# Average pooling by four: loads of 8 MiB with 64 KiB runs in two buffers, in place of 4 MiB with 32 KiB runs in four, and the wait for stores on the load queue

## Chip, cores, metric

One core of one Trainium2 chip. The metric is device time in microseconds (us), the median over several executions. In the profile's lines DVE is VectorE, ACT is ScalarE and POOL is GpSimd; SPq and ACTq are the queues on which SyncE and ScalarE issue DMAs; L70 is line 70 of that run's kernel.

## The reference

```python
x: (64, 256, 8192) float32, kernel_size = stride = 4
out[:, :, i] = mean(x[:, :, 4*i : 4*i+4], axis=2)      # (64, 256, 2048)
```

The program reads 536.87 MB and writes 134.22 MB. It has 16384 rows of 8192 numbers. Both kernels treat them as 32 groups of 128 partitions x 4 rows, so that the four rows of one partition lie next to each other in memory (128 KiB in, 32 KiB out).

## The kernel before

One row per partition is one load of 4 MiB (a 32 KiB run on each of 128 partitions). Four such buffers take the loads in turn. VectorE sums four numbers at a time, ScalarE multiplies by 1/4 in place, and when the four rows of a group are done, one store of 4 MiB (again 32 KiB per partition) goes out from ScalarE's queue. There are two result buffers of one group each, so before the first row of group g is written, the store of group g-2 must have landed: **VectorE** waits for that.

```python
# F = 4 rows per group, _NIN = 4 input buffers, _NOUT = 2 result buffers
def load(i):                                   # on SyncE's queue
    ld = nc.sync.dma_start(out=xbuf(i), in_=xrow(i))          # 128 x 32 KiB
    if i >= _NIN:
        ld._wait_ge(s_dve, i - _NIN + 1)       # buffer given back by VectorE
    ld.then_inc(s_in[i % _NIN], 16)
...
for i in range(NR):                            # VectorE
    g, f = divmod(i, F)
    if f == 0 and g >= _NOUT:
        nc.vector.wait_ge(s_out[g % _NOUT], 16 * (g // _NOUT))   # store g-2 landed
    nc.vector.tensor_reduce(out=..., in_=xbuf(i)..., op=add)
for i in range(NR):                            # ScalarE
    nc.scalar.mul(o, o, inv_k)._wait_ge(s_dve, i + 1).then_inc(s_act, 1)
    if g < NG - 2 and f == F - 1:
        store(nc.scalar, g)                    # 128 x 32 KiB
# ... the last two stores are shared between the two queues, the very last one cut in two
```

## Time and profile before

| | before |
|---|---|
| time | 1559.98 us (1559.95 to 1560.06, 3 runs) |
| DMA | 671.12 MB at a mean of 431 GB/s |
| VectorE / ScalarE busy | 71% / 16% |
| one group (4 loads + 1 store), steady | 48.5 us |

The page of the kernel before: busy time by engine, then the span in 40 slices (DMA is the busy share of the 16 DMA engines in tenths, 9 means 90% or more), the DMA queues (q1 is SyncE's, q10 is ScalarE's, q14 carries instructions; packets, MB, share of the engines' time), the chain of work that ended last, VectorE's reductions (busy us, mean ns of one, idle before them), and the DMA issues (KB each, median us from issue to landing).

```profile
DVE 1111.8 (71%) x128; ACT 245.7 (16%) x129; POOL 0.2 (0%) x4
...
DMA  9999999999999999999999999999999999999999
GB/s 407 427 431 431 431 435 435 436 431 431 431 431 435 434 434 431 431 431 431 434 437 433 431 431 431 431 437 434 434 431 431 431 431 436 434 434 431 431 431 392
DMA packets 23187, 671.12 MB, mean 431 GB/s; under 512 B 2576, under 2 KB 2576, under 8 KB 2576
...
q1 hardware_dynamic: 18720, 542.12, 80.8%
q10 hardware_dynamic: 4464, 128.98, 19.2%
q14 instruction: 3, 0.02, 0.0%
...
DMA 81%; DVE 18%; ACT 0%; issue 0%; SPq 0%
...
L92 DVE TENSOR_REDUCE res<-xin 128x2048 f32<-128x8192 f32 x128 | 1111.8, 8686 | 434.5 <-DMA xin<-in_x_dram 434.5
...
xin<-in_x_dram SPq DMA_DIRECT2D x128, 4096.0 KB, 39.8
out_dram<-res ACTq DMA_DIRECT2D x30, 4096.0 KB, 23.2
```

No slice drops below nine tenths, and the rate hardly moves: the DMA engines are the limit. The last two lines are the median times from issue to landing: 39.8 us for a load (it queues behind others) and 23.2 us for a store.

The whole waits of the DMA queue on SyncE, and of VectorE, in the kernel before (waiter, line, releaser: us in total, times, longest):

```profile
SPq L70 <- DVE res L92: 1462.3, 124, 18.9
```

```profile
DVE res L92 <- DMA xin<-in_x_dram: 434.5, 128, 13.0
```

The loads wait only for VectorE to give buffers back, and VectorE waits only for loads. The wait for the stores shows up nowhere: it is always over when it is reached.

**The packets.** The trace also records each DMA packet (start, duration, size, queue). In this trace one packet is one run of one partition: 32 KiB for loads and stores. I strung the packets together into 16 DMA engines by the rule that each starts where the previous one of its engine ended. On one of them, where a load and a store are both queued, it reads as follows. (This is my listing from the trace's records, start in us from the span's start, then duration.)

```
105.40 load 32 KiB 1213 ns     109.03 store 32 KiB 1213 ns
106.61 store 32 KiB 1213 ns    110.24 load 32 KiB 1213 ns
107.82 load 32 KiB 1213 ns     111.45 store 32 KiB 1213 ns
```

Most packets start 1.209 or 1.210 us after the one before. The Trainium skill (the notes on the chip), page "DMA: Bandwidth & Descriptors", section "Where 436 GB/s comes from", gives 435.2 GB/s as the ceiling, which is an estimated 1.205 us per 32 KiB and engine (435.2 GB/s shared by 16 engines); this trace is within 0.4% of it. A group needs 32 load and 8 store packets per engine, 40 x 1.209 = 48.4 us, against a measured period of 48.5 us. The same page, section "Queues, rings and completion order", says that each engine goes round-robin over the queues at packet granularity; the listing shows it, with a turn of exactly one 32 KiB packet.

### The profile page before, as it was taken

The numbers are of one execution on the slowest core, as the hardware profiler recorded it, in microseconds if no ns is written. First come the engines' busy times: TensorE is split into PE (matmuls) and PEld (weight loads), VectorE is DVE, ScalarE is ACT, GpSimd is POOL, SyncE is SP. The second block draws the span as 40 slices with busy tenths as digits, with TensorE's granted clock in tenths as the row PEclk, the third lists the DMA queues.
The fourth block names the chain that finished last, engine by engine and source line by source line (L and its number), as shares of the span: only waits on it lengthen the run. The fifth ranks groups of instructions, "written<-read, shape, count | busy, mean of one in ns | idle before, by whom it ended". The sixth has DMA issues, their size and how long they took to land.

```text
span 1558.4 us, 501 instructions
## 1 busy us (share of the span) xinstructions
DVE 1111.8 (71%) x128; ACT 245.7 (16%) x129; POOL 0.2 (0%) x4
## 2 busy tenths in 40 slices
DVE  6767667686677866777666776667866677666786
ACT  1111111111111111111111111111111111111111
POOL 0000000000000000000000000000000000000000
DMA  9999999999999999999999999999999999999999
GB/s 407 427 431 431 431 435 435 436 431 431 431 431 435 434 434 431 431 431 431 434 437 433 431 431 431 431 437 434 434 431 431 431 431 436 434 434 431 431 431 392
DMA packets 23187, 671.12 MB, mean 431 GB/s; under 512 B 2576, under 2 KB 2576, under 8 KB 2576
## 3 DMA queue, kind: packets, MB, share of 16 engines
q1 hardware_dynamic: 18720, 542.12, 80.8%
q10 hardware_dynamic: 4464, 128.98, 19.2%
q14 instruction: 3, 0.02, 0.0%
HBM read 536.87 MB, written 134.22 MB: 431 GB/s over the span
## 4 chain that ended last, share of the span: by engine, by line
DMA 81%; DVE 18%; ACT 0%; issue 0%; SPq 0%
DMA xin<-in_x_dram 81%; DVE res L92 18%; ACT res L102 0%; SPq L70 0%; SPq L140 0%; SPq L67 0%
## 5 line engine op out<-in xcount | busy, mean ns | idle before, releaser
L92 DVE TENSOR_REDUCE res<-xin 128x2048 f32<-128x8192 f32 x128 | 1111.8, 8686 | 434.5 <-DMA xin<-in_x_dram 434.5
L102 ACT ACTIVATE res<-res 128x2048 f32<-128x2048 f32 x128 | 244.4, 1909 | 1301.7 <-DVE res L92 1301.7
L102 ACT ACT_TABLE_LOAD x1 | 1.3, 1283 | 0.9 <-SPq L67 0.9
L126 POOL MEMSET const-bfloat16-1.0<- 128x1 bf16 x1 | 0.1, 101 | 0.0
L126 POOL MEMSET const-uint8-127<- 128x1 uint8 x1 | 0.1, 101 | 0.0
L126 POOL MEMSET const-float32-0.0<- 128x1 f32 x1 | 0.1, 98 | 0.2 <-issue 0.2
L126 POOL MEMSET const-float32-1.0<- 128x1 f32 x1 | 0.1, 98 | 0.0
## 6 DMA issues: line engine op xcount, KB each, us to landing
xin<-in_x_dram SPq DMA_DIRECT2D x128, 4096.0 KB, 39.8
out_dram<-res ACTq DMA_DIRECT2D x30, 4096.0 KB, 23.2
out_dram<-res SPq DMA_DIRECT2D x1, 4096.0 KB, 42.4
out_dram<-res ACTq DMA_DIRECT2D x1, 3072.0 KB, 16.6
out_dram<-res SPq DMA_DIRECT2D x1, 1024.0 KB, 8.7
```

Source lines behind the costliest of these rows:

```text
L92: nc.vector.tensor_reduce(out=obuf(g)[:, f * OL : (f + 1) * OL], in_=xbuf(i).rearrange("p (m k) -> p m k", k=K), axis=mybir.AxisListType.X ...
L102: nc.scalar.mul(o, o, inv_k)._wait_ge(s_dve, i + 1).then_inc(s_act, 1)
L126: nc = _bacc.Bacc("TRN2", target_bir_lowering=False, num_devices=1)
```

## The change

Intent: fewer and larger loads (8 MiB, 64 KiB per partition, so two rows per load), and fewer instructions. The kernel keeps two input buffers of 64 KiB per partition, the same bytes as the four before. To keep VectorE's instructions down, a wait moves off it: the load queue now waits for the store of group g-2 before it issues the first load of group g. Every second tile is summed in two passes of pairwise adds (in place into the input buffer, then into the results), which takes VectorE less time than one pass.

```diff
-_NIN = 4
+_R = 2          # rows per load
+_NIN = 2
...
-            ld = nc.sync.dma_start(out=xbuf(i), in_=xrow(i))
-            if i >= _NIN:
-                ld._wait_ge(s_dve, i - _NIN + 1)
-            ld.then_inc(s_in[i % _NIN], 16)
+            g, j = divmod(t, G)                       # G = 2 tiles per group
+            if j == 0 and r0 == 0 and g >= _NOUT:
+                nc.sync.wait_ge(s_out[g % _NOUT], 16 * (g // _NOUT))
+            ld = nc.sync.dma_start(
+                out=xbuf(t, r0, r1),
+                in_=xview(g)[:, (j * R + r0) * L : (j * R + r1) * L],
+            )
+            if t >= _NIN:
+                ld._wait_ge(s_dve, t - _NIN + 1)
+            ld.then_inc(s_last if r0 > 0 else s_in[t % _NIN], 16)
...
-            if f == 0 and g >= _NOUT:
-                nc.vector.wait_ge(s_out[g % _NOUT], 16 * (g // _NOUT))
-            nc.vector.tensor_reduce(...)              # one row
+            elif t % G == 0:
+                nc.vector.tensor_reduce(...)          # two rows, one pass
+            else:
+                half = xbuf(t)[:, : T // 2]
+                pairs(half, xbuf(t))._wait_ge(s_in[t % _NIN], landed).then_inc(s_half, 1)
+                pairs(obuf(t), half)._wait_ge(s_half, t // G + 1).then_inc(s_dve, 1)
# ... (cut: the last tile is still loaded and summed row by row; ScalarE multiplies two rows at a time)
```

## The prediction

> **What bounds the kernel now.** DMA. The page's slices show the DMA engines at nine tenths or more throughout and 431 to 437 GB/s; the chain that ended last is 81% loads and 18% VectorE. In order of time that chain repeats every 48.5 us (91.47, 139.95, 188.44 ...): one group of four 4 MiB loads and one 4 MiB store. VectorE is 71% busy (reductions of 8686 ns), ScalarE 16%; both wait on loads. The trace's single DMA packets explain the period: 32 KiB takes 1.21 us on each of 16 engines; 40 packets per engine and group make 48.4 us. The Trainium skill, "DMA: Bandwidth & Descriptors" (Where 436 GB/s comes from), gives a ceiling of 435.2 GB/s; this trace sits within 1% of it. So nothing more than about 10 us can be won.
>
> **What the change does.**
> - Loads of 64 KiB packets: a 32 KiB packet takes 1.209 us, 1.205 at the ceiling; halving the count saves an estimated 2 to 3 us in all. Fewer instructions save the instruction fetches; two of the three (544 and 581 us) stretched their periods by under 1 us together.
> - VectorE per 8 MiB: one pass an estimated 17.2 us (twice 8686 ns, less one fixed cost), two passes 8.7 + 4.4 = 13.1 us [...]. Both are under the 19.3 us of an 8 MiB load: VectorE stays off the bottleneck, even with two buffers.
> - The wait for the store of two groups back moves from VectorE (just before the overwriting) to the load queue, one whole load earlier: load 2g+4 can't be issued before store g has landed.
>
> **Why that matters.** Packets of load and store queues alternate one for one on an engine where both have work (trace: 1.21 us load, 1.21 us store, in turn), so a 4 MiB store lands 23.2 us after issue (median, part 6). The skill's page (Queues, rings and completion order) says that engines switch queues by packets; here a packet is one 32 KiB descriptor. If a 64 KiB run stays one packet, a turn is 2.41 + 1.21 us, and eight store packets take 29 us instead of 19.3.
>
> Timeline, A = landing of load 2g+1: VectorE done A+13.3, ScalarE A+17, store issued; first store packet 4 to 7 us later (4.4 now), behind packets already taken. Load 2g+3 started at about A+19, so the store ends with or after it. By then the load queue is empty: load 2g+4 waits for the store's semaphore, then needs about 0.4 us receipt, 1.2 to 1.6 us from issue to first packet, and 0.7 us of first-packet delay (seen at the kernel's start). Estimate: 1.3 to 3.3 us of idle DMA per group, 30 times: 40 to 100 us, all critical. Startup and tail add about 7 us.
>
> **Predicted:** 1628 us, range 1566 to 1658. Chances: faster 0.02, within 2% 0.20, slower 0.78.
>
> **What would show it.** DMA share of slices falls to about 0.95, GB/s to about 412; period 50 to 52 us per group; the load queue's own waits name the store (out_dram<-res) on the group-opening loads; store issue-to-landing rises from 23 to about 30 us; loads have about half the packets (some 8,200 of data); VectorE reductions 17.2 us, adds 8.7 and 4.4 us, VectorE busy falling to about 975 us.
>
> **What would make it wrong.** If 64 KiB runs are cut to 32 KiB packets, or turns go by bytes, the store lands in about 23 us, well before load 2g+4 is due, and the time is 1558 to 1570. If fewer packets are taken ahead, the idle halves (about 1600). If adds at step two run slower than one element a cycle, VectorE adds more.

## The result

The changed kernel took **1634.32 us** (1633.09 to 1637.35, 4 runs) against 1560.02 us (4 runs) in the same rounds. The ratio is 1.0479 (95% interval 1.0461 to 1.0497): slower. A ratio here is the mean time of one kernel's fast runs over that of the other's fast runs of the same rounds, so it is not quite the ratio of the medians quoted.

The page of the changed kernel, with the lines that answer to those shown of before, and the three VectorE groups (busy us, mean ns, idle before them):

```profile
DVE 974.9 (60%) x96; ACT 232.9 (14%) x66; POOL 0.2 (0%) x4
...
DMA  9989999999999999999899999999999999999999
GB/s 411 411 362 435 411 411 426 410 424 397 426 424 386 435 400 411 425 398 437 363 434 424 386 434 402 411 424 394 442 386 419 422 393 437 411 411 415 408 423 374
DMA packets 14115, 671.12 MB, mean 411 GB/s; under 512 B 1568, under 2 KB 1568, under 8 KB 1568
...
q1 hardware_dynamic: 9648, 542.12, 79.4%
q10 hardware_dynamic: 4464, 128.98, 18.4%
q14 instruction: 3, 0.02, 0.0%
...
DMA 73%; DVE 26%; ACT 0%; issue 0%; SPq 0%
...
L134 DVE TENSOR_REDUCE res<-xin 128x4096 f32<-128x16384 f32 x32 | 551.0, 17220 | 297.1 <-DMA xin<-in_x_dram 297.1
L105 DVE TENSOR_TENSOR xin<-xin 128x8192 f32<-128x8192 f32 x31 | 269.5, 8692 | 350.0 <-DMA xin<-in_x_dram 350.0
...
L105 DVE TENSOR_TENSOR res<-xin 128x4096 f32<-128x4096 f32 x31 | 137.2, 4425 | 1.1
...
out_dram<-res ACTq DMA_DIRECT2D x30, 4096.0 KB, 32.8
```

The same bytes move at 411 instead of 431 GB/s, and the rate swings from slice to slice. VectorE does less work than before (975 against 1112 us), so it isn't VectorE's throughput. A store now takes 32.8 us to land instead of 23.2. The share of busy DMA barely falls, because a packet that is held up counts as busy; the rate tells more here than the share.

The load queue's own waits, after:

```profile
SPq L81 <- DMA out_dram<-res: 1087.1, 30, 39.4
SPq L82 <- DVE res L105: 432.5, 31, 15.3
```

Line 81 is the moved wait. The loads now wait mainly for stores. A wait on the issuing queue costs nothing by itself (run e2 below waits 799 us and hardly loses by it); what counts is whether the DMA engines run dry meanwhile. That can be seen where the wait ends. The timeline of the changed kernel around one such place (start, duration, engine, line, work; in brackets the idle time before):

```profile
702.67 8.69 DVE L105 TENSOR_TENSOR xin<-xin 128x8192 f32<-128x8192 f32 x1 [12.38 <-DMA xin<-in_x_dram]
702.89 0.33 SPq L82 DMA_DIRECT2D xin<-in_x_dram  x1
```

At 702.67 VectorE starts on a load that has just landed; it was the last one in flight. The next load is issued only at 702.89, although its buffer had been free since 690.29, when the reduction on it ended. The packets and landings of one DMA engine around it (my listing from the trace's records, as above):

```
694.98 load 64 KiB 2418 ns
697.39 store 32 KiB 1213 ns
698.60 load 64 KiB 2418 ns      last packet of that load
701.02 store 32 KiB 1213 ns     last packet of the store, ends 702.23
702.65    load has landed (all 16 engines)
702.83    store has landed -> 702.89 next load issued
703.86 load 64 KiB 2961 ns      1.63 us without a packet, then a slow first one
 ...
718.90 load 64 KiB 2434 ns
719.50    the next store is issued
721.33 load 64 KiB 3765 ns      held up 1.35 us
725.09 store 32 KiB 1213 ns     first packet of that store
726.30 store 32 KiB 1213 ns
727.51 load 64 KiB 2418 ns
```

Loads and stores still take turns one packet for one packet, but a load packet is now twice as long. In these turns the eight store packets of a group stretch over eight load packets, which is a whole load. So store and load finish together, and the queue is empty while the store's landing, the issue and the first packet follow one another.

Added up over the whole trace, mean of the 16 DMA engines (the packets at their usual duration, the gaps over 50 ns between packets, and the excess of packets over the usual duration):

| | packets at usual length | gaps | excess in long packets | one group, steady |
|---|---|---|---|---|
| before | 1548.2 us | 0.0 us | 4.0 us | 48.53 us |
| after | 1546.0 us | 35.2 us | 45.4 us | 50.79 us |

Of the excess after, 11.3 us are the slow first packets behind a gap, and 28.2 us are the packets just before a store's first one (30 of them, 0.94 us each). So the stalled queue costs about 35.2 + 11.3 = 46 us, and the start of the stores about 28 us. This splits the loss by place, not by cause: in e1 below, without the wait, the part before a store's first packet falls from 28 to 12 us as well. From the trace, 15 of the 16.4 gaps per engine lie between a store packet and the first packets of a group's first load, the load that waits for the store. The periods alternate, 52.1 and 49.2 us: a stalled group delays its loads, so that the next store starts earlier in them and ends in time; one engine had 16 gaps in 32 groups. The "one group" column is the mean distance of 28 store issues.

### The profile page after: what moved, and what is told of

It reads as the page before. It is cut to its first block, busy times and chain, and to the rows that moved or that the text cites. A ratio compares the mean times of both kernels' runs of the same rounds, so it can differ in the third digit from the quotient of the medians.

```text
span 1631.3 us, 343 instructions
## 1 busy us (share of the span) xinstructions
DVE 974.9 (60%) x96; ACT 232.9 (14%) x66; POOL 0.2 (0%) x4
## 4 chain that ended last, share of the span: by engine, by line
DMA 73%; DVE 26%; ACT 0%; issue 0%; SPq 0%
DMA xin<-in_x_dram 71%; DVE xin L105 16%; DVE res L105 8%; DMA out_dram<-res 2%; DVE res L134 1%; DVE res L125 1%; ACT res L152 0%; SPq L82 0%; SPq L192 0%; SPq L81 0%; SPq L75 0%
## 5 line engine op out<-in xcount | busy, mean ns | idle before, releaser
L134 DVE TENSOR_REDUCE res<-xin 128x4096 f32<-128x16384 f32 x32 | 551.0, 17220 | 297.1 <-DMA xin<-in_x_dram 297.1
L105 DVE TENSOR_TENSOR xin<-xin 128x8192 f32<-128x8192 f32 x31 | 269.5, 8692 | 350.0 <-DMA xin<-in_x_dram 350.0
L152 ACT ACTIVATE res<-res 128x4096 f32<-128x4096 f32 (+1 forms) x65 | 231.6, 3564 | 1391.1 <-DVE res L134 733.9
L105 DVE TENSOR_TENSOR res<-xin 128x4096 f32<-128x4096 f32 x31 | 137.2, 4425 | 1.1
L125 DVE TENSOR_REDUCE res<-xin 128x2048 f32<-128x8192 f32 x2 | 17.3, 8676 | 0.0
## 6 DMA issues: line engine op xcount, KB each, us to landing
out_dram<-res ACTq DMA_DIRECT2D x30, 4096.0 KB, 32.8
```

What stands on the lines that cost most here:

```text
L105: return nc.vector.tensor_tensor(out=out, in0=v[:, :, 0], in1=v[:, :, 1], op=mybir.AluOpType.add)
L125: nc.vector.tensor_reduce(out=obuf(t, r, r + 1), in_=xbuf(t, r, r + 1).rearrange("p (m k) -> p m k", k=K), axis=mybir.AxisListType.X, op=m ...
L134: nc.vector.tensor_reduce(out=obuf(t), in_=xbuf(t).rearrange("p (m k) -> p m k", k=K), axis=mybir.AxisListType.X, op=mybir.AluOpType.add,) ...
L152: nc.scalar.mul(o, o, inv_k)._wait_ge(s_dve, t + 1 if t < NT - 1 else t + r1).then_inc(s_act, 1)
```

## The experiments

Theory: the wait for a store on the load queue, one load ahead of where the results are overwritten, together with the turns of one 64 KiB packet against one 32 KiB packet, empties the queue. Rivals: the moved wait costs this by itself; two buffers are too few for VectorE's time per tile; 64 KiB packets are slow in themselves. All eleven kernels were correct; there is no e6.

Runs e1 to e4 ran on one chip, e5 and e7 to e9 on a second, e10 to e12 on a third, each batch beside the kernel before (1559.97, 1559.99 and 1560.07 us; so close that times are compared across batches). Where packets are called long below, they take over 150 ns more than usual, counted per DMA engine.

### e1: the wait back on VectorE

```diff
-                nc.sync.wait_ge(s_out[g % _NOUT], 16 * (g // _NOUT))     # load queue
+            if t % G == 0 and t // G >= _NOUT:                           # VectorE
+                nc.vector.wait_ge(s_out[(t // G) % _NOUT], 16 * (t // G // _NOUT))
```

> The changed kernel with one thing undone: the wait for the store of two groups back stands again on VectorE, just ahead of the reduction that overwrites the results; loads of 64 KiB packets, two buffers and the sums by turns stay. Theory (the wait on the load queue, behind a store stretched by one-for-one turns with 64 KiB packets, empties the queue once a group): the gaps between packets go, time 1556 to 1566 us. But the changed trace also shows load packets that take 0.8 to 1.2 us longer just where a store starts; if those belong to 64 KiB packets and not to the stall, about 30 us stay and the time is 1585 to 1600. Rival (two buffers are too few, VectorE gives them back too late, wherever the wait stands): it stays at 1630 to 1640.

Measured: 1584.29 us (1577.88 to 1588.14), ratio 1.0151. The load queue's waits in this run:

```profile
SPq L79 <- DVE res L102: 776.4, 31, 26.2
SPq L79 <- DVE res L133: 734.6, 31, 38.2
```

And the landing of its stores:

```profile
out_dram<-res ACTq DMA_DIRECT2D x30, 4096.0 KB, 33.8
```

The load queue no longer waits for stores, though a store still takes as long to land (33.8 us). Gaps fell from 35.2 to 5.1 us. So the moved wait is worth 50 of the 74 us. The rest stayed, mostly as 26 us of excess in long packets, and the time is a hair under the second range. Of the 26 us, 12 sit just before a store's first packet and about 8 in load packets that take turns with a store. 64 KiB packets are not slow everywhere: they usually take 2418 ns, twice the 1.209 us of 32 KiB. Neither "all of it is the wait" nor "two buffers explain it all" holds.

### e2: the loads in packets of 32 KiB, wait left on the load queue

```diff
+            for r in range(r0, r1):
                 ld = nc.sync.dma_start(
-                    out=xbuf(t, r0, r1), in_=xview(g)[:, (j * R + r0) * L : (j * R + r1) * L])
+                    out=xbuf(t, r, r + 1), in_=xview(g)[:, (j * R + r) * L : (j * R + r + 1) * L])
# each of the two increments s_in by 16; VectorE waits for 32
```

> The changed kernel with each 8 MiB load issued as two loads of 32 KiB per partition; the wait stays on the load queue, two buffers of 8 MiB and the sums by turns stay. Theory: stores take turns with 32 KiB packets again and land about 23 us after issue, before the load that waits for them is due, so no gaps and no long packets at a store's start: 1558 to 1570 us. Rival one (the wait on the load queue costs this by itself, whatever the packets): 1630 to 1640. Rival two (two buffers are too few): 1630 to 1640.

Measured: 1572.35 us (1571.58 to 1577.93), ratio 1.0087, 2 us above the range. The DMA issues and the load queue's wait:

```profile
out_dram<-res ACTq DMA_DIRECT2D x30, 4096.0 KB, 23.6
```

```profile
SPq L81 <- DMA out_dram<-res: 799.0, 30, 27.5
```

With the packets halved, the store lands in 23.6 us again. (There are now also twice as many load issues. No run halves the packets alone, but 23.6 us is what turns of 32 KiB packets gave before.) The queue still waits 799 us for stores, but loads are still in flight meanwhile: gaps are 4.1 us. Undoing either half of the combination removes most of the loss.

### e7: both, the wait on VectorE and 32 KiB packets

The edits of e1 and e2 together.

> Two 32 KiB loads per tile and the wait back on VectorE, so that of the change only the two buffers of 8 MiB, given back whole, and the sums by turns are left. Theory: what run e2 still lost (12 us, in a few gaps and in load packets about 0.6 us longer where a store starts) belongs to the two buffers, because a load is issued only some 2 to 3 us before its first packet is due; so this equals e2 within 5 us: 1567 to 1577. Rival (the rest in e2 came from the wait on the load queue): 1558 to 1562.

Measured: 1570.66 us (1568.31 to 1571.70), ratio 1.0066, in the range. With the changed kernel this makes a square, which is the main result:

| | wait on the load queue | wait on VectorE |
|---|---|---|
| 64 KiB packets | 1634.3 us (after) | 1584.3 us (e1) |
| 32 KiB packets | 1572.4 us (e2) | 1570.7 us (e7) |

The wait on the load queue costs 50 us with 64 KiB packets. With 32 KiB packets the difference is 1.7 us, which the spread of these runs does not set apart from zero. All four have two buffers of 8 MiB and sums by turns.

### e3: the kernel before with only the wait moved

```diff
         def load(i):
+            g, f = divmod(i, F)
+            if f == 0 and g >= _NOUT:
+                nc.sync.wait_ge(s_out[g % _NOUT], 16 * (g // _NOUT))
# and the same wait taken off VectorE
```

> The kernel before with only the wait for the store moved from VectorE to the load queue, ahead of the first load of the group that will overwrite the results. Theory: with 32 KiB packets the store lands in 23 us, and with four buffers the queue holds several loads ahead, so the wait costs nothing: 1558 to 1564 us. Rival (the move of the wait alone is the cause): 1600 to 1640.

Measured: 1559.84 us, ratio 0.9999 (0.9984 to 1.0014). The move by itself costs nothing where packets are 32 KiB and four buffers keep loads queued.

### e4: one pass on every tile

```diff
-            elif t % G == 0:
+            elif True:              # tensor_reduce always; the two-pass branch goes
```

> The changed kernel with the two-pass sums replaced by one-pass reductions (17.2 us in place of 13.1 us on every second tile); all else stays. Theory: VectorE is not what limits, but the store of a group is issued about 4 us later, so that the stall can't shrink in any group: the time rises a little, 1636 to 1655 us. Rival (VectorE's time per tile is what holds up the loads): 4.1 us more in each of 31 groups, 1750 us or more.

Measured: 1664.95 us (1663.56 to 1668.74), ratio 1.0676, 10 us above the range. The rival's 1750 us is far off. The direction was as expected, but the expected size was too small: the store is issued 4 us later, and now every group stalls: 30.6 gaps per engine, 63.2 us in all, against 16.4 gaps and 35.2 us. The group takes 51.89 us. Of the 30.6 gaps, 30.0 lie between a store packet and the first packets of a group's first load. So VectorE matters here, but through the time at which the store leaves, not because loads wait for its buffers.

### e9: two passes on every tile, wait left on the load queue

```diff
-            elif t % G == 0:
-                nc.vector.tensor_reduce(...)
             else:
-                ... s_half, t // G + 1
+                ... s_half, t + 1
```

> The changed kernel with all sums in two passes; the wait stays on the load queue. Theory: VectorE's one-pass tiles are not what stalls the queue, the wait for the store is: it still stalls, 1605 to 1634 us. Rival (the one-pass tiles with two buffers are the cause): 1560 to 1580.

Measured: 1628.64 us (1627.92 to 1629.39), ratio 1.0440. In the range: the faster tiles take off 6 us and leave 32.2 us of gaps, still in every second group (the periods are 52.2 and 49.3 us). The one-pass tiles are not the cause.

### e5: the stores in packets of 16 KiB

```diff
-            eng.dma_start(out=oview(g)[:, f0 * OL : f1 * OL], in_=...)
+            for n, (c0, c1) in enumerate([(f0, F // 2), (F // 2, f1)]):     # full stores only
+                st = eng.dma_start(out=oview(g)[:, c0 * OL : c1 * OL], in_=...)
# ... counts of s_out doubled
```

> The changed kernel with each 4 MiB store issued as two stores of 16 KiB per partition, one right behind the other: twice the store packets, same bytes; all else stays. Theory: one-for-one turns by packets make the store last longer (sixteen store packets against eight load packets: landing 38 to 45 us after issue instead of 32.8), but packets that run after the loads are out still carry bytes, so only the empty queue's round trip is lost, now in every group instead of every second one: 1640 to 1670 us. Rival one (the loss grows with the time the store takes to land): 1700 us or more. Rival two (turns go by bytes): landing and time as in the changed kernel, 1630 to 1640.

Measured: 1661.87 us (1661.01 to 1663.11), ratio 1.0654, in the range. From the issue of the first half to the landing of both the store takes 38.5 us (median of the 30 stores, from the trace's landings), so the bytes are the same and the landing is later: turns go by packets, not bytes. Gaps are 31.8 per engine, 59.3 us. What is lost is one round trip per group, not the store's length; once every group stalls (as in e4), it hardly grows further.

### e8: e1 with two passes on every tile

The edits of e1 and e9 together.

> Run e1 (wait on VectorE, 64 KiB packets) with all sums in two passes, so that VectorE gives back every second buffer about 4 us earlier. Theory: the 24 us that e1 lost come from loads that are issued with almost no time to spare, so earlier release takes away a good part: 1562 to 1576 us. Rival (the 64 KiB packets lose it by themselves at each store's start): 1580 to 1590, as e1.

Measured: 1579.54 us (1575.04 to 1585.67), ratio 1.0128: between the two ranges, so it decides nothing by its time. The gaps went (5.1 to 0.6 us), and 18.9 us of long packets stayed. The profiled run was the fastest of the four (1575.04 us). Earlier release cures the gaps, and at most a part of the long packets (26 us in e1).

### e10: e7 with two passes on every tile

> Run e7 (32 KiB loads, wait on VectorE, two buffers of 8 MiB) with all sums in two passes, so that VectorE gives back every second buffer about 4 us earlier. Theory: the 11 us that e7 still loses come from loads issued with little time to spare: 1560 to 1567 us. Rival (they come from the start of the stores alone, as in e8, where the gaps went and the long packets stayed): 1567 to 1572, with gaps near none and 20 or more long load packets per DMA engine.

Measured: 1569.43 us (1567.73 to 1570.39), ratio 1.0059. The theory of this run fell and its rival held: gaps are 0.25 us, but 26 long load packets per engine stayed (13.1 us). So the 11 us that e7 loses are not loads that come too late.

### e11 and e12: the stores held back a little

The long packets sit just before a store's first packet. In the two-buffer kernels the store is issued just when one load passes to the next. Here ScalarE's queue waits for the next tile to land before it issues the store (e11 on e1, 64 KiB; e12 on e7, 32 KiB, with counts of 32):

```diff
             if g < NG - 2 and t % G == G - 1:
+                nc.scalar.wait_ge(s_in[(t + 1) % _NIN], 16 * ((t + 1) // _NIN + 1))
                 store(nc.scalar, g)
```

> Run e1 (wait on VectorE, 64 KiB packets) with each store held back on ScalarE's queue until the tile after its group has landed, about 2 to 3 us later, so that it starts two packets into a load and not where one load passes to the next. Theory: the long load packets at a store's start come from two cold starts together (a load just issued and a store just issued, with nothing else in the queue), so they go: 1562 to 1576 us. Rival (64 KiB packets lose it at every store's start, wherever it falls): 1580 to 1590, as e1.

> The same later store on run e7 (wait on VectorE, two 32 KiB loads per tile). Theory, as for e11: about 1560 to 1566 us. Rival: as e7, 1567 to 1572.

Measured: e11 1575.05 us (1572.52 to 1575.69), ratio 1.0091; e12 1562.81 us (1562.59 to 1563.03), ratio 1.0018 (1.0003 to 1.0033).

With 32 KiB packets the theory holds: long packets fall from 22 to 3.5 per engine, the group takes 48.50 us, as before, and 8 of the 11 us are back. With 64 KiB the time is inside the theory's range, at its upper edge, but the trace says otherwise: 30 long load packets per engine are still there, of which some 19 sit just before a store's first packet (11.6 us). So holding back the store won 9 us, and about 12 us (e11 minus e12) stay with the 64 KiB packets.

No version beat the kernel before: e3 equals it. The DMA engines of the kernel before have no gaps and 4 us of excess, so a faster version would have to move fewer bytes or raise the engines' rate.

## Why the prediction was right, point by point

- **What bounds the kernel, and that little could be won: right.** The larger packets saved 1548.2 - 1546.0 = 2.2 us, predicted 2 to 3.
- **VectorE's costs: right.** 17220, 8692 and 4425 ns against 17.2, 8.7 and 4.4 us, which follow from the reduction before (8686 ns for 8192 numbers, 1.06 ns each); busy 974.9 against 975 us. The Trainium skill, "VectorE: DVE Perf Modes" (the errata section), gives (N + 151) / 0.96 ns for an fp32 add; for 8192 and 4096 that is an estimated 8690.6 and 4424 ns. The trace agrees, though these operands step by two.
- **Turns by packet, 64 KiB as one packet, a late store: right.** 8064 packets of 64 KiB; store landing 32.8 us, predicted about 30; the load queue waits for out_dram<-res, as predicted; e5 shows the turns go by packets.
- **The stall: right in kind, its term was over-counted.** I charged 1.3 to 3.3 us of idle in each of 30 groups, some 60 us in the predicted total. The trace shows it in every second group, 35.2 us of gaps and 11.3 us of slow first packets per engine: 46 us, or 2.8 us for each of 16.4 stalls. So the size of one stall was right and the count was wrong: the prediction overlooked that a stalled group lets the next store end in time. Taking away the wait (e1) won 50 us.
- **A term was missing: the start of a store.** Load packets just before a store's first packet are held up, 28 us in all after, against none in the steady groups before. The predicted total came out right, 1628 against 1634 us, because the over-counted term and the missing one nearly cancelled. That closeness is luck: a right total does not prove a right sum. The packet account does the splitting here, by place; e1 gives what the wait is worth, 50 us. The 7 us that I added for startup and tail were not measured apart.
- **Fewer instructions would save the instruction fetches: wrong.** The page shows three instruction packets in both kernels (q14).
- **DMA share about 0.95: wrong as a sign.** Stretches of the changed run show 0.97 to 0.99, as held-up packets count as busy; the rate (411 GB/s, predicted 412) was the right sign.

What stays open: why a load packet is held up when a store starts near it, and why 64 KiB packets suffer it even where the store starts inside a load (e11). The runs show when it happens, not the mechanism.

## What to carry to other kernels

When two DMA queues share the engines, compare their packet sizes, not only their bytes: here, doubling the load packets made the stores land after 32.8 us in place of 23.2 us, and everything that waited for them shifted. Before moving a wait onto the queue that feeds the bottleneck, ask how much work is still queued behind it when it ends; with four buffers the same move cost nothing, with two and longer packets it cost 50 us. A DMA share near 1.0 does not show a full rate: read GB/s and the period of one group.

## What the Trainium skill lacked or had wrong

- "DMA: Bandwidth & Descriptors" (Queues, rings and completion order) says that a turn is a packet, typically of about 9 to 17 descriptors. Here a turn was one run, of 16, 32 or 64 KiB, and a store of eight 32 KiB packets per engine landed in 23.2 us against 32 KiB load packets and 32.8 us against 64 KiB ones. The page does not warn of unequal runs.
- The same page's rules ask for at least 1 MiB per DMA and name no upper end. Loads of 8 MiB with 64 KiB runs saved 2.2 us of packet time, and cost 13.6 us against two 4 MiB loads into the same buffers (e1 against e7).
- No page has the hold-up of load packets at a store's start: 0.94 us each, 30 times, in the changed kernel; with 32 KiB packets and the store issued later it was gone (e12).
- "Runtime: NRT & Kernel Launch" (Instruction fetch mechanics) speaks of refills in blocks of 16 KiB. The three instruction packets inside the span were of 8 KiB each and came at least 36 us apart, in both kernels, with 501 and with 343 instructions.
